# Conditioning columns in groups of four, parked FFN loads asked for earlier, and one operation for the FFN input's scale: a hybrid attention and SSD block on one core

## The chip, the cores and the metric

The kernel runs on one core of a Trainium2 chip. Five engines work side by side, each with its own queue: TensorE (PE, with its weight loads as PEld), VectorE (DVE), ScalarE (ACT), GpSimd (POOL) and SyncE (SP), whose queue here issues the DMAs. SBUF holds the tiles, PSUM the banks into which TensorE sums. The metric is the device time of one execution in microseconds; lower is better.

## The reference

One layer over x of 1024 rows and 1024 columns, all in float32. `mod` holds six vectors of 1024, made from a conditioning vector.

```python
mod = (jax.nn.silu(c) @ ada_w + ada_b)[:, None, :]
shift_m, scale_m, gate_m, shift_f, scale_f, gate_f = jnp.split(mod, 6, axis=-1)
h = rmsnorm(x, pre_norm_mix) * (1.0 + scale_m) + shift_m
proj = h @ w_in
...
y_a = sparse_mla_attention(q_lat, kv_lat, k_idx, w_idx, positions, ...) @ w_o_attn
y_b = ssd_mixer(z, xbc, dt_raw, ...) @ w_o_ssd
mix = (jax.nn.sigmoid(g_a) * y_a + jax.nn.sigmoid(g_b) * y_b) @ w_out
x = x + gate_m * rmsnorm(mix, post_norm_mix)
h2 = rmsnorm(x, pre_norm_ffn) * (1.0 + scale_f) + shift_f
u_gate, u_up = jnp.split(h2 @ w_ffn_in, 2, axis=-1)
f = (jax.nn.silu(u_gate) * u_up) @ w_ffn_out
x = x + gate_f * rmsnorm(f, post_norm_ffn)
```

The attention scores all keys with an indexer, keeps the best 256 per query and attends to these; the SSD mixer is a causal convolution of width 4 and a chunked scan.

## The kernel before

**Products.** Activations lie transposed: 128 channels in the partitions, rows in the free dimension, in two halves of 512 (`half(b)`, b = 0 and 1). A float32 product is made of split operands: hi is the rounded float32r copy (made by ACT), lo the rest (made by DVE or POOL), and three matmuls (hi with hi, lo with hi, hi with lo) add into one PSUM bank. Weights come through a stream of 128 x 4 x 128 pieces: SP loads wraw, ACT makes whi (L149), POOL makes wlo (L150), TensorE uses both.

**What sets the order.** The kernel is traced by Python, and a scheduler then orders each engine's queue by a simulated timetable. Under `in_order` a part keeps the written order on the named engines: TensorE through most of the attention, and again from the second half's output projection to the end of the early FFN tiles. Tiles lie in arenas of fixed slots (EV has 9 slots of 128 x 512, H 32, Q 26); a slot is given again when the last reader of its old tile is done. `bank_d` is a rotation of three PSUM banks, shared by the products pw, pos, pot, p2 and by adap.

**The conditioning columns.** `mod` has 48 columns of 128. Columns 16 to 47 are made beside the attention: `ada_slow` loads two adaw tiles of 256 KB, POOL multiplies both by the vector cs (L314) and adds them (L316), DVE reduces them to a tile adas of 128 x 128 (L318). `ada_next` keeps three columns waiting, and then `ada_col` multiplies one adas tile with a column of ones into a bank (L283), from which DVE adds the bias into `mod` (L284). Beside them stand `pw`, the products with w_in, whose convolution on DVE (cv, L892 to L894) reads two banks at a time.

**Merge and output projection.** `merge(b)` makes for each of eight blocks t a product pos with w_o_ssd; DVE multiplies it (mrg, L1138), POOL multiplies it by the gate (L1139), DVE adds the attention's part yal (L1142), and ACT and DVE split it into mg (L243, L244). `mixed(b)` multiplies the eight mg with w_out into pot. Then come the residual, the second normaliser and the FFN's input for this half.

**FFN input.** `residual_steps` ends with x1 times pr2, the normaliser spread over the partitions in PSUM (L1186). `ffn_input(b)` applies scale am2 and shift mod[24 + t]: for half 0 ACT makes h2h from x1 (L1195), DVE makes h2 in place (xr, L1196), and h2l is the difference (L1198, in turn on POOL and DVE). For half 1 only L1196 runs. Half 0's input is made during the last pos products of `merge(1)` and the first pot products.

**FFN tiles.** The FFN's first product uses Strassen's sums over four quarters. `early` makes the first products of 16 tiles (tile t's first half goes as p1, its gate part as g0, to a parking place d_p1 in DRAM) while the second half's residual is made; the list `fill` is this generator, `EARLY` is 16. `gate_up(t)` then does the rest of each tile: it loads four weight tiles a11, a12, a21, a22, loads the parked p1 and g0 (L1293, L1294), makes s1 and s2 (L1301, L1302), multiplies ("2", "1", "3", "22") and adds p1 into g1 (L1308). Weights become wr by ACT and POOL (L1251, L1252).

Of the kernel before, what the change touches and what calls it, by code (L numbers as in the profile page):

```python
# [10 lines left out]
F32 = mybir.dt.float32  # L11
F32R = mybir.dt.float32r
BF = mybir.dt.bfloat16
AF = mybir.ActivationFunctionType
OP = mybir.AluOpType
AX = mybir.AxisListType

P = 128
# [9 lines left out]
FT = D_FF // P  # L28
# [37 lines left out]
def build(tc, a, dbg=None, stop=99, slots=None):  # L66
    nc = tc.nc
    V, S, G, T, SP = nc.vector, nc.scalar, nc.gpsimd, nc.tensor, nc.sync
# [3 lines left out]
    con = ctx.enter_context(tc.tile_pool(name="con", bufs=1))  # L72
# [6 lines left out]
    EV = Arena(ctx, tc, "EV", n_slots["EV"], 512)  # L79
# [4 lines left out]
    def bank_d(name):  # L84
        return pd.tile([P, 512], F32, name=name, tag="d", bufs=3)

    def bank(name):
        return ps.tile([P, 512], F32, name=name, tag="s", bufs=5)

    def f(x):  # L90
        return x.bitcast(F32)
# [87 lines left out]
    def col(name, j=0, n=1):  # L179
        o, _ = COLS[name]  # L180
        return vec[:, o + j:o + j + n]
# [10 lines left out]
    onec = ones[:, 0:1]  # L192
# [15 lines left out]
    d_p1 = dr.tile([EARLY, 2, P, 512], F32, name="d_p1")  # L208
# [69 lines left out]
    mod = con.tile([P, 48], F32, name="mod")  # L278
    amul = con.tile([P, 8], F32, name="amul")

    def ada_col(j, acc):
        p = bank_d("adap")
        T.matmul(p[:, 0:1], acc, onec, start=True, stop=True)  # L283
        V.tensor_tensor(mod[:, j:j + 1], p[:, 0:1], col("ada_b", j), op=OP.add)  # L284

    cs32 = sm.tile([P, 8, 32], F32, name="cs32", tag="r2", bufs=1)
    V.memset(cs32, 0.0)
# [17 lines left out]
        V.tensor_tensor(mod[:, k:k + 9:8], p[:, 0:2], vec[:, k:k + 9:8], op=OP.add)  # L305
        V.scalar_tensor_tensor(amul[:, k:k + 1], mod[:, 8 + k:9 + k], 1.0, col("pre_mix", k), op0=OP.add, op1=OP.mult)

    def ada_slow(j):

        ts = []  # L310
        for h in range(2):
            t = wp.tile([P, 4, P], F32, name="adaw", tag="adaw", bufs=2)
            behind(SP.dma_start(t, a["ada_w"][j - 16][:, 4 * h:4 * h + 4]))
            behind(G.tensor_tensor(t, t, cs[:, 4 * h:4 * h + 4, None].to_broadcast([P, 4, P]), op=OP.mult))  # L314
            ts.append(t)
        G.tensor_tensor(ts[0], ts[0], ts[1], op=OP.add)  # L316
        acc = EV("adas", (P, P))
        V.tensor_reduce(acc, ts[0].rearrange("p k m -> p m k"), axis=AX.X, op=OP.add)  # L318
        return j, acc

    AHEAD = 4
    X0 = [[None, None] for _ in range(KT)]
    rx, Hs, first = [None, None], [([None, None], [None, None]) for _ in range(KT)], {}
# [62 lines left out]
    with in_order(*ORDERED, mybir.EngineType.SP):  # L386
        sums = [None, None], [None, None]
# [26 lines left out]
        for k in range(2, KT):  # L414
            k_h(k, 0)
            k_h(k, 1)
            if AHEAD <= k + 2 < KT:
                i = k_load(k + 2).ins
# [44 lines left out]
    for b in BS:  # L463
# [5 lines left out]
        hi, lo = Q("ksh", dt=F32R), Q("ksl", dt=F32R)  # L469
# [84 lines left out]
    acc = {i: (Q if i < 4 else R)(f"acc{i}") for i in range(QT0, NT)}  # L554
    for c in range(8):
# [5 lines left out]
        for hh in range(2):  # L561
            o, oo = 64 * hh, 64 - 64 * hh
            qs = []
            for b in BS:
                t = Q("qs", dt=F32R)
# [6 lines left out]
        for hh in range(2):  # L572
            qs = qss[hh]
            hd = 2 * c + hh
            for i in range(QT0, NT):
                n = (i + 1) * P
# [24 lines left out]
    for x in range(2):  # L601
# [3 lines left out]
        for j in range(NT):  # L605
# [3 lines left out]
            t = Q("v")  # L609
# [107 lines left out]
    if dbg is not None and "mk" in dbg:  # L717
        for i in MK:
            n = (i + 1) * P
            t = R("t")  # L720
# [175 lines left out]
            S.activation(ts[b], ts[b], AF.Silu)  # L896
            SP.dma_start(dst[:, half(b)], ts[b])

    slow, late = iter(range(16, 48)), []

    def ada_next():

        j = next(slow, None)
        if late and (j is None or len(late) > 2):
            ada_col(*late.pop(0))
        if j is not None:
            late.append(ada_slow(j))

    def group(g):
        return (16 + g, d_bc[g, 0]), (24 + g, d_bc[g, 1]), (2 * g, d_xs[2 * g]), (2 * g + 1, d_xs[2 * g + 1])  # L910
# [2 lines left out]
    for kind in FILL:  # L913
# [3 lines left out]
        elif kind == "z":  # L917
            t = next(n_z)
            gate(1 + t, d_z[t], AF.Silu)
        elif stop != 3:  # L920
            t = next(n_a)
# [177 lines left out]
    if stop <= 3:  # L1099
        for k in range(16):  # L1100
            for b in BS:
                t = EV("ydump")
# [9 lines left out]
    am2 = con.tile([P, 8], F32, name="am2")  # L1112
# [50 lines left out]
    def residual_steps(b, mix, sacc, x1):  # L1163

        r = rstd([sacc], D)
        yield
        prm = rspread(r)
        sacc = None
        for t in range(8):
            xr = Q("xr")  # L1170
            SP.dma_start(xr, a["xT"][t][:, half(b)])
            V.scalar_tensor_tensor(mix[t], mix[t], gm[:, t:t + 1], prm, op0=OP.mult, op1=OP.mult)
            (V if t % 2 else G).tensor_tensor(xr, mix[t], xr, op=OP.add)
            sq = mix[t]
            S.activation(sq, xr, AF.Square)
            if t:
                V.tensor_tensor(sq, sq, sacc, op=OP.add)
            sacc = sq
            x1.append(xr)
            SP.dma_start(d_x1[t][:, half(b)], xr)  # L1180
        yield
        r = rstd([sacc], D)
        yield
        pr2 = rspread(r)
        for t in range(8):
            V.tensor_tensor(x1[t], x1[t], pr2, op=OP.mult)  # L1186
        yield

    def ffn_input(b, x1):

        for t in range(8):
            h2 = x1[t]
            if b == 0:
                hi, lo = H_("h2h", dt=F32R), H_("h2l", dt=F32R)
                S.activation(hi, h2, AF.Identity, bias=mod[:, 24 + t:25 + t], scale=am2[:, t:t + 1])  # L1195
            V.tensor_scalar(h2, h2, am2[:, t:t + 1], mod[:, 24 + t:25 + t], op0=OP.mult, op1=OP.add)  # L1196
            if b == 0:
                (V if t % 2 else G).tensor_tensor(lo, h2, f(hi), op=OP.subtract)  # L1198
                X[("11", "21")[t // 4]][t % 4] = hi, lo
        return x1  # L1200


# [31 lines left out]
    x1 = []  # L1234
    for _ in residual_steps(0, *mixed(0, MG), x1):
        pass
    MG = merge(1, in_r)
    x1 = ffn_input(0, x1)


# [3 lines left out]
    def w_load(part, name, t, h):  # L1244
        r = w_tile(part, name)
        SP.dma_start(r, a["w_ffn_in"][t][:, 4 * h:4 * h + 4])
        return r
# [23 lines left out]
    def early(ts):  # L1271

        for t in ts:
# [10 lines left out]
            SP.dma_start(d_p1[t, 1], g)  # L1284
            yield

    def gate_up(t):

        a11, a12 = w_load(0, "a11", t, 0), w_load(0, "a12", t, 1)
        a21, a22 = w_load(1, "a21", FT + t, 0), w_load(1, "a22", FT + t, 1)  # L1290
        if t < EARLY:
            p, p1, g0 = bank("p0"), EV("p1"), EV("g0")
            SP.dma_start(p1, d_p1[t, 0])  # L1293
            SP.dma_start(g0, d_p1[t, 1])  # L1294
        else:
            p, g0, p2 = first_two(a11, a12)
            p1 = None
            V.tensor_tensor(g0, p2, g0, op=OP.add)
            S.activation(g0, g0, AF.Silu)
        s1, s2 = w_tile(2, "s1"), w_tile(2, "s2")  # L1300
        V.tensor_tensor(s1, a21, a22, op=OP.add)  # L1301
        V.tensor_tensor(s2, s1, a11, op=OP.subtract)  # L1302
        product(p, w_parts(s2), "2", p1 is not None)
        g1 = EV("g1")
        if p1 is None:
            S.activation(g1, p, AF.Copy)
        else:
            V.tensor_tensor(g1, p, p1, op=OP.add)  # L1308
        p5 = bank("p5")
        product(p5, w_parts(s1), "1", True)  # L1310
        u1 = EV("u1")
        if p1 is None:
            S.activation(u1, p5, AF.Copy)
        else:
            V.tensor_tensor(u1, p5, p1, op=OP.add)
        V.tensor_tensor(a21, a11, a21, op=OP.subtract)
        product(p, w_parts(a21), "3", False)
        V.tensor_tensor(u1, p, u1, op=OP.add)
        V.tensor_tensor(a12, a12, s2, op=OP.subtract)
        product(p5, w_parts(a12), "22", False)  # L1320
        V.tensor_tensor(g1, p5, g1, op=OP.add)
        S.activation(g1, g1, AF.Silu)
        top, j = t % 2 == 0, t // 2
        b12, t1 = kept[:, j % 2, 0], kept[:, j % 2, 1]
        last = b12 if top else g1
        V.tensor_tensor(last, g1, u1, op=OP.mult)
        if not top:
            SP.dma_start(d_a[PRODUCT["3"], j], g1)
            V.tensor_tensor(b12, g1, b12, op=OP.subtract)
            SP.dma_start(d_a[PRODUCT["7"], j], b12)  # L1330
            V.tensor_tensor(t1, g1, t1, op=OP.subtract)
            SP.dma_start(d_a[PRODUCT["6"], j], t1)
        product(p, w_parts(a22), "4", False)
        if p1 is None:
            V.tensor_tensor(g0, p, g0, op=OP.mult)
        else:
            V.tensor_tensor(p1, p, p1, op=OP.add)
            V.tensor_tensor(g0, g0, p1, op=OP.mult)
        if top:
            SP.dma_start(d_a[PRODUCT["1"], j], g0)  # L1340
            V.tensor_tensor(t1, b12, g0, op=OP.subtract)
            SP.dma_start(d_a[PRODUCT["5"], j], t1)
        else:
            SP.dma_start(d_a[PRODUCT["2"], j], g0)
            V.tensor_tensor(u1, g0, t1, op=OP.subtract)
            SP.dma_start(d_a[PRODUCT["4"], j], u1)

    kept = con.tile([P, 2, 2, 512], F32, name="kept", tag="mk")

    with in_order(mybir.EngineType.PE):  # L1350
        mix, sacc = mixed(1, MG)
        y1 = []
        fill, rest = early(range(EARLY)), residual_steps(1, mix, sacc, y1)
        for n in (2, 1, 7, 2):
            for _ in range(n):
                next(fill)
            next(rest)
        next(rest, None)
        ffn_sums(x1, ffn_input(1, y1))
        for _ in fill:  # L1360
            pass
    for t in range(FT):
        gate_up(t)

# [104 lines left out]
    with in_order(mybir.EngineType.PE, mybir.EngineType.Activation, mybir.EngineType.DVE,  # L1469
# [27 lines left out]
        for i, (name, j) in enumerate(steps):  # L1497
            n = ORDER.index(name)
# [14 lines left out]
            hi, lo = (alloc("a" + k, None, F32R) for k in "hl" for alloc in [(H_, Q)[PRODUCT[nxt] % 2]])  # L1513
# [23 lines left out]
        for c in BS:  # L1537
            cl, sacc = slice(256 * c, 256 * c + 256), None
            for m in range(4):
                p = bank("pfl")[:, 0:256]  # L1540
# [108 lines left out]
```

## Time and profile before

| what | value |
|---|---|
| time, median of 3 runs | 2430.15 us (2428.41 to 2433.94) |
| profiled execution | 2432.21 us |
| its span | 2430.3 us |
| mean granted TensorE clock | 0.991 |
| TensorE busy | 2352.2 us, 97% of the span |
| DVE, ACT, POOL busy | 65%, 50%, 44% |

The profiled execution takes 1.9 us more than its span, which is what lies around the recorded instructions. An engine's busy time is the sum of its instructions; what an engine waits for is told by the waits, which name the operation whose end released it. Times within the span are counted from its start.

### The profile page before, as it was taken

What the parts mean: (1) busy time and instruction counts of PE and PEld (TensorE: products, weight loads), DVE (VectorE), ACT (ScalarE), POOL (GpSimd) and SP (SyncE); (2) the same over time, 40 slices, a digit from 0 to 9 for tenths busy, and PEclk for the clock granted to TensorE, in tenths of its full rate; (3) what the DMA queues carried; (4) which work ended last, traced back from release to release, by engine and by line L of the source; (5) the groups of instructions that cost most, each with busy time, mean ns of one, the idle gap of its engine ahead of it and who ended that gap; (6) DMA issues with size and microseconds to landing.
All of it is one profiled execution on the core that took longest, in us unless ns stands there. A gap on an engine that the chain in (4) does not pass through costs nothing. (4 is left out here: it accounts for less than half of the span.)

```text
span 2430.3 us, 35062 instructions
## 1 busy us (share of the span) xinstructions
PE 2352.2 (97%) x11878; PEld 1909.0 (79%) x11878; DVE 1572.8 (65%) x3077; ACT 1226.1 (50%) x2336; POOL 1074.3 (44%) x854
## 2 busy tenths in 40 slices
PE   7999999999999999999999999999899999999997
PEld 5888888887888787777776777887777888887877
DVE  4466775598765566675557677354376877547776
ACT  4456665567455555455566565453444222335442
POOL 1422112222243446651345435666567555444465
PEclk9999999999999999999999999999999999999999
DMA  7123122522322223322668885554364555328664
GB/s 271 66 88 122 66 74 79 161 100 87 104 85 94 90 98 107 109 77 92 206 218 286 273 270 178 185 196 143 107 236 156 187 175 199 106 97 303 220 216 162
DMA packets 227651, 369.85 MB, mean 152 GB/s; under 512 B 22624, under 2 KB 84752, under 8 KB 227472
## 3 DMA queue, kind: packets, MB, share of 16 engines
q1 hardware_dynamic: 226752, 367.03, 45.1%
q8 instruction: 94, 1.54, 0.3%
q14 instruction: 85, 0.70, 0.1%
q10 hardware_dynamic: 720, 0.58, 0.1%
HBM read 275.74 MB, written 94.92 MB: 153 GB/s over the span
## 5 line engine op out<-in xcount | busy, mean ns | idle before, releaser
L150 POOL TENSOR_TENSOR wlo<-wraw,whi 128x512 fp32r<-128x512 f32 x242 | 331.4, 1371 | 612.6 <-ACT whi L149 558.2
L1258 PE MATMUL p<-xh,wr 128*128 128x512 f32 x880 | 276.6, 392 | 5.7 <-DVE g L1308 4.1
L149 ACT ACTIVATE whi<-wraw 128x512 fp32r<-128x512 f32 x242 | 151.1, 627 | 228.8 <-issue 58.0
L1252 POOL TENSOR_TENSOR wr<-a,wr 128x512 fp32r<-128x512 f32 x110 | 157.4, 1439 | 126.6 <-ACT wr L1251 94.0
L1258 PEld LDWEIGHTS p<-xh,wr 128*128 128x128 f32 x880 | 166.6, 189 | 41.7 <-DVE g L1308 4.6
L1258 PE MATMUL p<-xl,wr 128*128 128x512 f32 x440 | 172.2, 391 | 0.0
L778 ACT ACTIVATE lg<-lg,mx 128x256 f32<-128x256 f32 (+7 forms) x128 | 98.6, 772 | 93.8 <-DVE mx L775 91.5
L1251 ACT ACTIVATE wr<-a 128x512 fp32r<-128x512 f32 x110 | 68.4, 629 | 143.4 <-PE p L1258 120.8
L1258 PE MATMUL p<-h2h,wr 128*128 128x512 f32 x352 | 112.4, 395 | 0.0
L638 ACT ACTIVATE junk<-acc,cand__2182 128x1024 bf16<-128x1024 f32 (+2 forms) x96 | 86.2, 898 | 45.8 <-DVE cand__2182 L681 29.9
L314 POOL TENSOR_TENSOR adaw<-adaw,cs 128x512 f32<-128x512 f32 x64 | 66.3, 1041 | 90.5 <-DMA adaw<-ada_w 78.5
L1430 PE MATMUL pfo<-ah,wlo 128*128 128x512 f32 x264 | 103.4, 392 | 2.3 <-POOL wlo L244 2.3
L223 PE MATMUL pos<-yh,wlo 128*128 128x512 f32 x256 | 101.2, 396 | 2.8 <-POOL wlo L150 2.7
L1430 PE MATMUL pfo<-ah,whi 128*128 128x512 f32 x264 | 103.1, 390 | 0.7 <-ACT whi L243 0.7
L589 DVE SCALAR_TENSOR_TENSOR acc<-rel,widx,acc 128x384 f32<-128x384 f32 (+2 forms) x90 | 87.1, 988 | 24.9 <-ACT rel L584 24.7
L1430 PE MATMUL pfo<-al,whi 128*128 128x512 f32 x264 | 102.7, 389 | 0.0
L223 PE MATMUL pos<-yh,whi 128*128 128x512 f32 x256 | 101.1, 396 | 1.2 <-ACT yh L1124 1.2
L584 ACT ACTIVATE rel<-prel 128x512 f32<-128x512 f32 (+3 forms) x160 | 77.2, 523 | 48.5 <-PE prel L583 44.9
L223 PE MATMUL pos<-yw,whi 128*128 128x512 f32 x256 | 100.5, 393 | 0.0
L1258 PEld LDWEIGHTS p<-xl,wr 128*128 128x128 f32 x440 | 83.4, 189 | 17.3
L1519 DVE TENSOR_TENSOR al<-al,ah 128x512 fp32r<-128x512 f32 x66 | 73.1, 1110 | 36.1 <-ACT ah L1514 35.6
L799 PE MATMUL pt<-ident,lg 128*128 128x128 f32 x576 | 87.9, 277 | 4.0 <-ACT pc L804 2.1
(581 smaller groups left out, 7178.9 us busy)
## 6 DMA issues: line engine op xcount, KB each, us to landing
wraw<-w_in SPq DMA_DIRECT2D x130, 256.0 KB, 2.6
a<-w_ffn_in SPq DMA_DIRECT2D x120, 256.0 KB, 3.2
al<-d_a SPq DMA_DIRECT2D x77, 256.0 KB, 4.2
wraw<-w_ffn_out SPq DMA_DIRECT2D x66, 256.0 KB, 3.7
adaw<-ada_w SPq DMA_DIRECT2D x64, 256.0 KB, 2.7
al<-d_ac SPq DMA_DIRECT2D x32, 512.0 KB, 5.3
wraw<-w_o_ssd SPq DMA_DIRECT2D x64, 256.0 KB, 2.8
d_a<-kept SPq DMA_DIRECT2D x33, 256.0 KB, 3.0
```

The costliest lines, as they stand in the source:

```text
L149: behind(S.activation(hi[:, :kt], raw[:, :kt], AF.Copy))
L150: behind(G.tensor_tensor(lo[:, :kt], raw[:, :kt], f(hi[:, :kt]), op=OP.subtract))
L223: T.matmul(o, wt[:, k0 + i, :], xs[k][xi][b][:, sl], start=pi == 0 and i == 0 and wt is hi and xi == 0, stop=pi == len(pcs) - 1 and i == l ...
L584: S.activation(rel[:, 512 * b:512 * b + w_], pr[:, 0:w_], AF.Relu)
L589: V.scalar_tensor_tensor(acc[i][:, 0:n], rel[:, 0:n], ws, acc[i][:, 0:n], op0=OP.mult, op1=OP.add)
L638: S.activation(jk, y, AF.Sign, scale=-1.0, bias=a_, accum_out=o)
L778: S.activation(lg[:, 0:n], lg[:, 0:n], AF.Exp, scale=-1.0, bias=m, accum_out=mx[:, 3:4])
L799: T.transpose(ptv[:, hh, t, :], PR[hh, t][:, j * P:(j + 1) * P], ident)
L1252: G.tensor_tensor(w[:, 1], src, f(w[:, 0]), op=OP.subtract)
L1258: T.matmul(p, w[:, wi, i], X[x][i][xi], start=start and i == 0 and k == 0, stop=i == 3 and k == 2, skip_group_check=True)
L1430: T.matmul(o, w[wi][:, P * m:P * m + P], x[xi][:, cl], start=j == 0 and k == 0, stop=j == NP - 1 and k == 2)
L1519: V.tensor_tensor(lo, r, f(hi), op=OP.subtract)
```

## The change

Three edits.

1. Modulation columns end in fours. A tile of 128 x 4 x 128 in EV (first[j]) takes the reductions of four columns; `ada_cols` then makes four matmuls into one bank and one DVE add over four columns of `mod`. A group ends two columns after its last column is reduced.
2. `up_loads`, `parked` and `gate_loads` take the loads of `gate_up` out, and for tile 0 they are called behind steps 13, 15 and 17 of what is left of `fill`, beside the early tiles. `ahead` hands them on.
3. `residual_steps` multiplies by am2 and pr2 in one operation (a scalar_tensor_tensor, STT). `ffn_input` makes h2h with the shift alone on ACT, h2l on DVE alone (an STT that adds the shift and subtracts h2h), and h2 in place on ACT. The tensor_scalar of L1196 is gone.

```diff
-    def ada_col(j, acc):
+    def ada_cols(j, acc):
         p = bank_d("adap")
-        T.matmul(p[:, 0:1], acc, onec, start=True, stop=True)
-        V.tensor_tensor(mod[:, j:j + 1], p[:, 0:1], col("ada_b", j), op=OP.add)
+        for i in range(4):
+            T.matmul(p[:, i:i + 1], acc[:, i], onec, start=i == 0, stop=i == 3, skip_group_check=True)
+        V.tensor_tensor(mod[:, j:j + 4], p[:, 0:4], col("ada_b", j, 4), op=OP.add)
...
-    def ada_slow(j):
+    def ada_slow(j, acc):
...
-        acc = EV("adas", (P, P))
         V.tensor_reduce(acc, ts[0].rearrange("p k m -> p m k"), axis=AX.X, op=OP.add)
-        return j, acc
...
-    slow, late = iter(range(16, 48)), []
+    slow, sums = iter(range(16, 48)), {}
...
-        if late and (j is None or len(late) > 2):
-            ada_col(*late.pop(0))
+        if sums and (j is None or j % 4 == 2):
+            ada_cols(*sums.popitem())
         if j is not None:
-            late.append(ada_slow(j))
+            if j % 4 == 0:
+                first[j] = EV("adas", (P, 4, P))
+            acc = first[j - j % 4]
+            ada_slow(j, acc[:, j % 4])
+            if j % 4 == 3:
+                sums[j - 3] = acc
...
-            V.tensor_tensor(x1[t], x1[t], pr2, op=OP.mult)
+            V.scalar_tensor_tensor(x1[t], x1[t], am2[:, t:t + 1], pr2, op0=OP.mult, op1=OP.mult)
...
-                S.activation(hi, h2, AF.Identity, bias=mod[:, 24 + t:25 + t], scale=am2[:, t:t + 1])
-            V.tensor_scalar(h2, h2, am2[:, t:t + 1], mod[:, 24 + t:25 + t], op0=OP.mult, op1=OP.add)
-            if b == 0:
-                (V if t % 2 else G).tensor_tensor(lo, h2, f(hi), op=OP.subtract)
+                S.activation(hi, h2, AF.Identity, bias=mod[:, 24 + t:25 + t])
+                V.scalar_tensor_tensor(lo, h2, mod[:, 24 + t:25 + t], f(hi), op0=OP.add, op1=OP.subtract)
                 X[("11", "21")[t // 4]][t % 4] = hi, lo
+            S.activation(h2, h2, AF.Identity, bias=mod[:, 24 + t:25 + t])
...
+    def up_loads(t):
+        return w_load(1, "a21", FT + t, 0), w_load(1, "a22", FT + t, 1)
+
+    def gate_loads(t):
+        return w_load(0, "a11", t, 0), w_load(0, "a12", t, 1)
+
+    def parked(t):
+        p1, g0 = EV("p1"), EV("g0")
+        SP.dma_start(p1, d_p1[t, 0])
+        SP.dma_start(g0, d_p1[t, 1])
+        return p1, g0
...
-        a11, a12 = w_load(0, "a11", t, 0), w_load(0, "a12", t, 1)
-        a21, a22 = w_load(1, "a21", FT + t, 0), w_load(1, "a22", FT + t, 1)
+        a11, a12 = ahead.pop((gate_loads, t), None) or gate_loads(t)
+        a21, a22 = ahead.pop((up_loads, t), None) or up_loads(t)
...
-            p, p1, g0 = bank("p0"), EV("p1"), EV("g0")
-            SP.dma_start(p1, d_p1[t, 0])
-            SP.dma_start(g0, d_p1[t, 1])
+            p, (p1, g0) = bank("p0"), ahead.pop((parked, t), None) or parked(t)
...
-        for _ in fill:
-            pass
+        for i, _ in enumerate(fill):
+            for n, fn in ((13, up_loads), (15, parked), (17, gate_loads)):
+                if i == n:
+                    ahead[fn, 0] = fn(0)
```

What it moves in the queues, at the places that the prediction speaks of. First SP in the attention, beside the convolution (wraw are weight loads, adaw the column loads, d_att, d_bc stores of rb and cv). Before:

```order
L897 DMA d_bc_104<-cv_7008 128x512
L313 DMA adaw_7437<-ada_w 128x512
L148 DMA wraw_7678<-w_in 128x512
L820 DMA d_att_101<-rb_7177 128x256
L313 DMA adaw_7440<-ada_w 128x512
L148 DMA wraw_7898<-w_in 128x512
L313 DMA adaw_7663<-ada_w 128x512
L897 DMA d_bc_104<-cv_7205 128x512
```

After:

```order
L896 DMA d_bc_104<-cv_7002 128x512
L314 DMA adaw_7427<-ada_w 128x512
L314 DMA adaw_7430<-ada_w 128x512
L314 DMA adaw_7649<-ada_w 128x512
L314 DMA adaw_7652<-ada_w 128x512
L314 DMA adaw_7872<-ada_w 128x512
L314 DMA adaw_7875<-ada_w 128x512
L148 DMA wraw_7663<-w_in 128x512
L819 DMA d_att_101<-rb_7168 128x256
```

Six column loads now stand ahead of the weight load and the store of rb. This is so at two places of the attention; elsewhere four stand in a row at most.

Second DVE between the last two mrg of the second merge and the last mg. Before (xr is h2 of half 0):

```order
L1138 TENSOR_TENSOR mrg_16470<-pos_16397,rys_14669 128x512
L1196 TENSOR_SCALAR xr_15810<-xr_15810,am2_14553,mod_117 128x512
L1196 TENSOR_SCALAR xr_15816<-xr_15816,am2_14553,mod_117 128x512
L1142 TENSOR_TENSOR mrg_16470<-mrg_16470,yal_16476 128x512
L1198 TENSOR_TENSOR h2l_16573<-xr_15816,h2h_16572 128x512
L1196 TENSOR_SCALAR xr_15823<-xr_15823,am2_14553,mod_117 128x512
L244 TENSOR_TENSOR mg_16479<-mrg_16470,mg_16479 128x512
...
L1196 TENSOR_SCALAR xr_15844<-xr_15844,am2_14553,mod_117 128x512
L1198 TENSOR_TENSOR h2l_16593<-xr_15844,h2h_16592 128x512
L1138 TENSOR_TENSOR mrg_16555<-pos_16482,rys_14669 128x512
```

After:

```order
L1142 TENSOR_TENSOR mrg_16398<-pos_16325,rys_14597 128x512
L1200 SCALAR_TENSOR_TENSOR h2l_16496<-xr_15738,mod_117,h2h_16495 128x512
L1200 SCALAR_TENSOR_TENSOR h2l_16501<-xr_15744,mod_117,h2h_16500 128x512
L1200 SCALAR_TENSOR_TENSOR h2l_16506<-xr_15751,mod_117,h2h_16505 128x512
L1146 TENSOR_TENSOR mrg_16398<-mrg_16398,yal_16404 128x512
L1200 SCALAR_TENSOR_TENSOR h2l_16511<-xr_15758,mod_117,h2h_16510 128x512
L244 TENSOR_TENSOR mg_16407<-mrg_16398,mg_16407 128x512
L1200 SCALAR_TENSOR_TENSOR h2l_16516<-xr_15765,mod_117,h2h_16515 128x512
L1200 SCALAR_TENSOR_TENSOR h2l_16521<-xr_15772,mod_117,h2h_16520 128x512
L1142 TENSOR_TENSOR mrg_16483<-pos_16410,rys_14597 128x512
```

Six h2l stand between the two mrg where six L1196 and three L1198 stood; two more follow behind the second mrg, each ahead of a step of its mg. POOL has no h2l any more, and ACT has the eight in-place operations between its weight halves.

Third SP at the end of the early tiles. Before:

```order
L1246 DMA a22_17940<-w_ffn_in 128x512
L1284 DMA d_p1_109<-g0_17724 128x512
L1246 DMA a12_18049<-w_ffn_in 128x512
L1278 DMA d_p1_109<-p1_17751 128x512
L1246 DMA a11_18155<-w_ffn_in 128x512
L1246 DMA a21_18051<-w_ffn_in 128x512
L1284 DMA d_p1_109<-g0_17767 128x512
L1278 DMA d_p1_109<-p1_17794 128x512
L1293 DMA p1_17835<-d_p1_109 128x512
L1294 DMA g0_17836<-d_p1_109 128x512
```

After:

```order
L1249 DMA a22_17868<-w_ffn_in 128x512
L1298 DMA p1_17672<-d_p1_109 128x512
L1299 DMA g0_17673<-d_p1_109 128x512
L1287 DMA d_p1_109<-g0_17656 128x512
L1249 DMA a12_17977<-w_ffn_in 128x512
L1281 DMA d_p1_109<-p1_17687 128x512
```

The parked loads of tile 0 stand directly behind the a22 load of tile 1, seven places earlier. Tile 0's own a11, a12, a21 and a22 stood ahead of this place before, too.

More of the change, by code (lines that the diff above doesn't have):

```diff
@@ L1346, in gate_up @@
             SP.dma_start(d_a[PRODUCT["4"], j], u1)
-    kept = con.tile([P, 2, 2, 512], F32, name="kept", tag="mk")
+    kept, ahead = con.tile([P, 2, 2, 512], F32, name="kept", tag="mk"), {}
     with in_order(mybir.EngineType.PE):
```

## The prediction

> **What bounds the kernel now.** I read the page first, then the waits of TensorE, then the stretches around its long waits, then the rows of the engine that it waited for.
>
> ```profile
> span 2430.3 us, 35062 instructions
> PE 2352.2 (97%) x11878; PEld 1909.0 (79%) x11878; DVE 1572.8 (65%) x3077; ACT 1226.1 (50%) x2336; POOL 1074.3 (44%) x854
> ```
>
> TensorE (PE) is busy 97% of the span; 2430.3 - 2352.2 = 78.1 us are idle. The change removes no product, so it can win only these idle microseconds and the time that matmuls run slow behind them. The profiled execution took 2432.21 us (1.9 us around its span), 2.1 us more than the median 2430.15; I take the sum off the median.
>
> Who ends PE's waits, in the three stretches that the change touches (attention in written order, 650 to 900; attention left to the scheduler, 900 to 1146; from the end of the second merge into the FFN, 1690 to 1880):
>
> ```profile
> PE pw L233 <- DVE mod L284: 4.6, 4, 1.3
> PE pw L233 <- DVE cv L893: 0.4, 2, 0.2
> ...
> PE plg L766 <- DVE mx L775: 5.9, 5, 1.6
> ...
> PE p L1258 <- DVE g L1308: 4.1, 1, 4.1
> PE p L257 <- DVE mix L1177: 4.1, 1, 4.1
> PE pot L223 <- ACT mg L243: 3.8, 1, 3.8
> PE pot L223 <- DVE mg L244: 2.5, 1, 2.5
> PE p L1258 <- POOL wr L1252: 0.9, 1, 0.9
> PE p L1258 <- ACT wr L1251: 0.7, 1, 0.7
> ```
>
> (Total, times, longest.) A long wait costs more than itself, as the stretches of 5 us show; the number in brackets behind PE's busy time counts matmuls, and the third value from the end is the granted clock:
>
> ```profile
> 1715.00:1720.00 5.00, 2.78 (x7) 2.23 (x8) 2.16 (x2) 1.60 (x3) 2.21 (x2) 0.56 0.16 53
> 1720.00:1725.00 5.00, 5.00 (x18) 4.01 (x17) 0.00 (x0) 0.63 (x1) 1.37 (x2) 0.75 0.16 52
> 1725.00:1730.00 5.00, 5.00 (x24) 4.14 (x23) 0.92 (x1) 2.24 (x4) 2.16 (x2) 1.00 0.34 108
> ...
> 1870.00:1875.00 5.00, 5.00 (x12) 3.98 (x13) 3.19 (x5) 0.00 (x0) 0.00 (x0) 0.50 0.60 196
> 1875.00:1880.00 5.00, 5.00 (x21) 4.03 (x21) 1.84 (x3) 1.71 (x3) 2.54 (x2) 0.89 0.17 65
> ```
>
> At full clock 5 us hold 23 to 24 matmuls, about 0.215 us each. From 1720 to 1725 only 18 ran (1.2 us lost), and the 2.8 us busy before that held 7 instead of 13 (1.2): about 2.4 us behind the merge's waits. From 1870 to 1880 33 ran instead of 46 to 47, of which 13 x 0.215 = 2.8; say 2.5 belong to the 4.1 us wait.
>
> [...]
>
> **The change part by part.**
>
> *Ada columns by four.* Before, every column takes a bank of the rotation of three (bank_d) and gives it back by a mod add that stands in DVE's order behind the convolution. Afterwards two groups stand in the stretch 650 to 900, where the 4th and the 8th column stood. The four waits of 4.6 us fell at the 1st, 3rd, 5th and 7th column, where no group takes a bank any more; at the 4th and 8th PE waits 0.2 for cv, which stays. If the freed waits only move to the next product, half comes back; bounds 2.3 to 4.6. I take 4.2, since the next product's bank is then one turn older. The matmuls stay 64 records, the mod adds fall from 32 to 8 on a DVE that is 65% busy, nothing on the path. In 900 to 1146 the scheduler orders PE anew around the removed matmuls; the longest total there, 5.9 above, comes from the attention's own softmax, which stays. I take 0, with bounds of 4 us either way, two thirds of that wait.
>
> The loads move on SP: six adaw loads stand in a row where they stood singly between other transfers. I cost that at nothing; the cover is in these rows:
>
> ```profile
> SPq L148 <- POOL wlo L150: 135.8, 27, 12.4
> L316 POOL TENSOR_TENSOR adaw<-adaw 128x512 f32<-128x512 f32 x11 | 14.2, 1294 | 0.7
> L318 DVE TENSOR_REDUCE adas<-adaw x11: 1042/1068/1095, 688.5 to 892.6; 128x128 f32<-128x512 f32 x11
> L314 POOL TENSOR_TENSOR adaw<-adaw,cs 128x512 f32<-128x512 f32 x21 | 21.9, 1041 | 41.8 <-DMA adaw<-ada_w 35.4 <-DVE cv L894 4.8 <-DVE cv L892 1.7
> adaw<-ada_w SPq DMA_DIRECT2D x64, 256.0 KB, 2.7
> L819 DVE TENSOR_TENSOR rb<-po,rb x10: 413/417/425, 706.0 to 897.7; 128x256 f32<-128x256 f32 x10
> ```
>
> SP waits 135.8 of 245 us for weights to be consumed anyway, so weight loads stand far ahead. A column's round is 2.7 (landing) + 2 x 1.04 + 1.29 + 1.07 = 7.1 us, and six loads (two buffers) hold SP about two rounds, 14 us. What stands behind them is a d_att store of rb, whose single buffer is written again after (897.7 - 706.0) / 9 = 21.3 us. 7 us are left.
>
> *FFN input.* Rows of the end of the second merge: two of DVE, four of PE, then a stretch between the two mrg, and what the new forms cost elsewhere.
>
> ```profile
> 1694.81 0.69 DVE L1138 TENSOR_TENSOR mrg<-pos,rys 128x512 f32<-128x512 f32 x1 [5.38 <-PE pos L223]
> 1709.47 0.68 DVE L1138 TENSOR_TENSOR mrg<-pos,rys 128x512 f32<-128x512 f32 x1
> ...
> 1705.49 0.62 PE L223 MATMUL pot<-mg,whi 128*128 128x512 f32 x2
> 1710.02 0.39 PE L223 MATMUL pot<-mg,wlo 128*128 128x512 f32 x1
> 1714.20 0.50 PE L223 MATMUL pot<-mg,whi 128*128 128x512 f32 x1 [3.79 <-ACT mg L243]
> 1717.22 0.80 PE L223 MATMUL pot<-mg,whi 128*128 128x512 f32 x1 [2.52 <-DVE mg L244]
> ...
> 1695.45:1709.47 14.02, 14.02 (x63) 11.61 (x63) 13.20 (x13) 9.89 (x15) 12.10 (x8) 1.00 0.40 130
> ...
> L1196 DVE TENSOR_SCALAR xr<-xr,am,mod x16: 533/543/1519, 1696.1 to 1810.5; 128x512 f32<-128x512 f32 x16
> L1198 DVE TENSOR_TENSOR h2l<-xr,h2h 128x512 fp32r<-128x512 f32 x4 | 6.6, 1651 | 0.2
> L1125 DVE SCALAR_TENSOR_TENSOR yw<-yl,vec,yh x32: 734/751/1831, 1438.2 to 1591.6; 128x512 fp32r<-128x512 f32 x32
> L1172 DVE SCALAR_TENSOR_TENSOR mix<-mix,gm,prn x16: 740/742/748, 1624.5 to 1772.7; 128x512 f32<-128x512 f32 x16
> L1186 DVE TENSOR_TENSOR xr<-xr,prn x16: 678/680/689, 1659.0 to 1805.7; 128x512 f32<-128x512 f32 x16
> L1195 ACT ACTIVATE h2h<-xr,mod,am x8: 799/802/817, 1695.3 to 1706.0; 128x512 fp32r<-128x512 f32 x8
> L364 ACT ACTIVATE h2h<-x,mod x2: 722/724/725, 40.4 to 42.6; 128x512 fp32r<-128x512 f32 x2
> ```
>
> PE was through the last pos and began pot at 1705.5, but DVE came to the last mrg at 1709.47: nine operations of L1196 and L1198 stood ahead of it. POOL, DVE, ACT and DVE then made mg in turn, with two more of these operations before mg lo. Alone, DVE's work between the two mrg is 6 x 0.53 + 3 x 0.68 + yal and mg lo at 0.68 = 6.6 us (0.68 is the fastest two-operand row, L1186); it filled 13.2, beside eight POOL operations of about 1.3 (L316 above), 10.4: each us of POOL cost DVE 0.64. Afterwards six h2l STTs, yal and mg lo are 6 x 0.75 + 1.4 = 5.9, beside five POOL operations (three h2l are gone), 6.5: 5.9 + 0.64 x 6.5 = 10.1. So the mrg can start at 1695.5 + 10.1 = 1705.6, just as PE delivers; POOL takes 1.5, yal ends at 1709, ACT's mg at 1710, and mg lo, behind the last h2l, at 1711. PE wants it from 1710.4: a wait of 0.6 for 6.3, and no slow clock. Gain 5.7 + 2.4 = 8.1. Bounds: 8.7 with no wait; with every STT at L1125's slowest, 6 x 1.8 + 1.4 = 12.2, mrg is at 1707.7, the wait 2.2 and half the slow clock stays, 5.3.
>
> ACT loses 8 x 0.08 (0.80 to 0.72) and gains seven identities of 0.72, which follow each other every 0.65 or so, in these 14 us: 9.9 - 0.6 + 4.6 = 13.9. It is just full, so the weight halves come about 1 us later; PE holds more than one piece (2.7 us of matmuls) ahead, and I cost that at nothing. It is the thinnest cover of the sum.
>
> L1186 as STT costs 16 x 0.06 (0.742 against 0.680), in stretches where PE is fed by pot or early tiles. In the second half eight L1196 leave DVE just ahead of the FFN's sums, which start earlier; that counts only for the 1.6 us of the next part. The wait for L1177 stays.
>
> *Loads of main tile 0.*
>
> ```profile
> 1855.85 0.33 SPq L1246 DMA_DIRECT2D a<-w_ffn_in  x1
> 1864.39 0.43 SPq L1293 DMA_DIRECT2D p<-d_p  x1
> ...
> 1869.14 0.69 DVE L1308 TENSOR_TENSOR g<-p,p 128x512 f32<-128x512 f32 x1 [4.42 <-DMA p<-d_p]
> 1869.89 0.80 PE L1258 MATMUL p<-xh,wr 128*128 128x512 f32 x1 [4.13 <-DVE g L1308]
> ```
>
> The parked p1 is asked for at 1864.39 and used at 1869.14, 4.75 us later. Now its load stands directly behind the a22 load issued at 1855.85: used from 1861, g1 at 1861.7, before PE comes at 1869.89 - 4.13 = 1865.8, less what else was saved. The 4.1 and its 2.5 go. The 0.9 and 0.7 hang on s2 of tile 1, behind the FFN's sums; I take half, 0.8. The parked g0 behind p1 takes a slot that a DVE operation of an early tile gives back, done well before by the rotation; the two loads pass four stores and three weight loads, which come 0.4 us of issue later for each. Gain 7.4; bounds 8.2, and 4.1 if the next tile's load makes PE wait for half of it.
>
> Sum: 4.2 + 0 + 8.1 + 7.4 = 19.7; 2430.15 - 19.7 = 2410.5, said as 2411. All lower bounds together: 2.3 - 4 + 5.3 + 4.1 = 7.7 (2422); all upper: 4.6 + 4 + 8.7 + 8.2 = 25.5 (2405).
>
> **The rivals.**
>
> (A) *Slower: six adaw loads block SP.* If the columns keep the pace of before, 245 / 11 = 22.3 us, two rounds hold SP 44.6, and rb's next write waits 23.3 us on DVE, with the convolution and PE behind it; at two such places 46.6: 2411 + 46.6 = 2458. It outweighs the gain from rounds of (21.3 + 9.9) / 2 = 15.6 us. Against it: the operations themselves make 7.1.
>
> (B) *The merge stays bound by DVE or ACT.* If STT and POOL never overlap, 5.9 + 6.5 = 12.4 us and mrg is at 1707.9, mg lo at about 1713.2: a wait of 2.8 for 6.3, with half the slow clock, 3.4 us less gain, 2414; if ACT also falls 3 us behind, 2417. For it: L1198's mean of 1.65. [...] The stretch above goes against taking it in full: 13.2 busy us of DVE and 12.1 of POOL lay in 14.0, though the waits may be inside those busy times.
>
> (C) *Another wait takes the place of p1's*, for a22 or wr of tile 1 or for the next parked tile: the gain there is 3 for 7.4, 2415.
>
> (D) *The new order costs in 900 to 1146* and the columns win nothing: 19.7 - 4.2 - 4 = 11.5, 2419; with (C) 2423.
>
> **How the numbers follow.** Main case 0.55, 2411, its own range 2405 to 2417; B 0.12, C 0.10, D 0.13, A 0.10 (from a small block, 2425, to 2458). 0.2%, 4.9 us, is about what measurement tells from no change: faster is below 2425.3, slower above 2435. A gives half of itself to slower and half to the same, D with C a little to the same: faster 0.88, same 0.07, slower 0.05. From 2404 to 2425 lies about 0.85 of the chance; below 2404 more than all upper bounds would be needed.
>
> **What would show it.** Right: PE's waits for mod fall from 4.6 to about 0; mrg of the last pos starts within 1 us of PE's last pos, and no clock under 0.9 from 1700 to 1720; L1308's counterpart runs about 4 us before PE needs it, and 1860 to 1880 holds 0.9 or more. Wrong: a wait of PE for cv or rb of more than 3 us between 750 and 900 (A), mg still 2 us or more late (B), a wait for DMA p1 or a (C), or a sum of waits above 15 us in 900 to 1146 (D).

## The result, and the profile after

The changed kernel took 2417.56 us (median of 6 runs) against 2431.76 us for the kernel before beside it: a ratio of 0.9946, 95% interval 0.9931 to 0.9960, so 9.7 to 16.8 us faster. The prediction was 2411, 19.7 us faster, with a range of 2404 to 2425. The time fell by some two thirds of that.

The page after, its first rows:

```profile
span 2415.7 us, 35058 instructions
PE 2349.2 (97%) x11878; PEld 1907.3 (79%) x11878; DVE 1555.6 (64%) x3041; ACT 1234.1 (51%) x2352; POOL 1068.9 (44%) x850
```

TensorE is idle for 2415.7 - 2349.2 = 66.5 us, 11.6 less than before, and 3.0 us less busy with the same matmuls, which fits less slow clock behind long waits (mean granted clock 0.992 for 0.991). The waits of TensorE after, in the same three stretches (line numbers have moved by -1 in the attention, by 2 to 5 from the merge to the early tiles, by 13 in `gate_up`):

```profile
PE plg L765 <- DVE ql L737: 1.6, 3, 1.1
...
PE plg L765 <- DVE mx L774: 6.2, 6, 1.7
...
PE p L257 <- DVE mix L1181: 3.6, 1, 3.6
PE p L1261 <- DVE u L1328: 2.3, 1, 2.3
PE pot L223 <- DVE mg L244: 1.1, 1, 1.1
PE pot L223 <- ACT mg L243: 0.6, 1, 0.6
```

The waits for mod, for g and for wr are gone. Two have come: for ql in the attention, and for u at the FFN's begin.

Where the time went is read best from the start of each matmul in two traces. I matched the matmuls of both in order and took how much later or earlier the same one starts; the change of that shift over a stretch is what the stretch lost or won. The table has it for every kernel of this study against the profile of before, in us, with the stretches by the time of before. Each column is one profiled execution, and so is the profile of before: what that one lost or won by chance stands in every column. "ratio" is that of the timed runs.

| stretch | after | e1 | e2 | e3 | e4 | e7 | e8 | e10 | e11 | e12 |
|---|---|---|---|---|---|---|---|---|---|---|
| columns in | 4s | 4s | - | - | - | 4s | eight | eight | - | - |
| loads early | yes | - | yes | - | yes | yes | yes | yes | - | yes |
| FFN input new | yes | - | - | yes | yes | yes | yes | yes | yes | - |
| orders on DVE set | - | - | - | - | - | u1, mg | - | u1, mg | u1 | u1 |
| 0 to 660 | +1.3 | +0.9 | +0.1 | -1.6 | +0.8 | +0.6 | -1.3 | +3.0 | +0.7 | +0.9 |
| 660 to 900 | -3.1 | -3.3 | 0.0 | 0.0 | 0.0 | -3.7 | -4.1 | -4.1 | -0.1 | 0.0 |
| 900 to 1146 | +1.0 | +1.3 | -0.4 | -0.2 | -0.1 | +1.7 | +0.8 | +1.9 | +0.4 | -0.1 |
| 1146 to 1690 | -0.1 | -3.3 | -0.4 | -1.1 | +3.4 | -0.5 | +3.7 | +0.2 | -1.6 | +0.3 |
| 1690 to 1736 (merge) | -7.1 | -0.4 | -0.5 | -7.1 | -5.5 | -7.6 | -5.4 | -7.6 | -7.0 | +0.2 |
| 1736 to 1857 | -0.6 | -0.6 | -0.2 | -0.3 | -0.7 | +0.1 | -0.6 | -0.4 | -0.2 | +0.1 |
| 1857 to 2100 (FFN) | -6.8 | -1.8 | -2.5 | -5.3 | -6.6 | -9.5 | -7.1 | -9.5 | -5.4 | -7.5 |
| 2100 to the end | +0.8 | -0.4 | +2.0 | -1.0 | -0.1 | 0.0 | +0.1 | -0.8 | -0.2 | -1.1 |
| sum | -14.6 | -7.6 | -1.9 | -16.5 | -8.8 | -18.9 | -13.9 | -17.4 | -13.4 | -7.2 |
| ratio | 0.9946 | 0.9996 | 0.9993 | 0.9965 | 0.9950 | 0.9932 | 0.9939 | 0.9923 | 0.9953 | 0.9972 |

Rows 0 to 660, 1146 to 1690 and 2100 to the end hold nothing of the change but eight operations of the residual's new form from 1658 on, and they scatter by -3.3 to +3.7 us. So a column's sum says little (e1's is -7.6 where its timed runs show about none). The rows with the change repeat better between kernels that are alike there: -5.3 and -5.4, or -6.8, -6.6 and -7.1, or -9.5 and -9.5 at the FFN's begin. But they scatter too: the merge gives 7.1 and 5.4 with the same operations, and e1's FFN row shows -1.8 with none of the change in it. Both come mostly from the clock (1.6 of the 1.7 us between the two merges, 1.5 of e1's 1.8); the scatter has its own section at the end.

The rows that answer to the prediction's places. DVE and then PE at the end of the second merge:

```profile
1704.99 0.68 DVE L1142 TENSOR_TENSOR mrg<-pos,rys 128x512 f32<-128x512 f32 x1
1707.51 1.75 DVE L1146 TENSOR_TENSOR mrg<-mrg,yal 128x512 f32<-128x512 f32 x1 [1.19 <-POOL mrg L1143]
1709.19 1.75 DVE L1200 SCALAR_TENSOR_TENSOR h2l<-xr,mod,h2h 128x512 fp32r<-128x512 f32 x1
1710.87 0.68 DVE L244 TENSOR_TENSOR mg<-mrg,mg 128x512 fp32r<-128x512 f32 x1
...
1709.98 0.51 PE L223 MATMUL pot<-mg,whi 128*128 128x512 f32 x1 [0.56 <-ACT mg L243]
1711.61 0.50 PE L223 MATMUL pot<-mg,whi 128*128 128x512 f32 x1 [1.12 <-DVE mg L244]
```

The mrg starts at 1704.99; on the clock of before (this trace is 1.0 us ahead there) that is 1706.0, 3.5 us earlier than the 1709.47 of before. That is 0.7 us after the start of PE's last pos matmul (1704.28): the queue of FFN inputs hardly holds it any more. What is left is the way behind it: yal took 1.75 and the last h2l, which stands ahead of mg lo, another 1.75.

SP, DVE and PE at the FFN's begin:

```profile
1845.29 0.42 SPq L1298 DMA_DIRECT2D p<-d_p  x1
1855.47 1.59 SPq L1249 DMA_DIRECT2D a<-w_ffn_in  x2
...
1852.95 0.68 DVE L1321 TENSOR_TENSOR g<-p,p 128x512 f32<-128x512 f32 x1
1858.16 0.69 DVE L1314 TENSOR_TENSOR s<-a,a 128x512 f32<-128x512 f32 x1 [4.53 <-DMA a<-w_ffn_in]
1860.16 0.68 DVE L1328 TENSOR_TENSOR u<-p,p 128x512 f32<-128x512 f32 x1
...
1860.89 0.50 PE L1261 MATMUL p<-xh,wr 128*128 128x512 f32 x1 [2.29 <-DVE u L1328]
```

The parked p1 is asked for at 1845.29 and g1 is ready at 1853.6, with no wait. But DVE then stood 4.5 us at s1 of tile 2, whose a22 load was issued only at 1855.47, and u1 of tile 0 stood behind it in DVE's queue. That everything was there for u1 by then is shown by e7 below, where it ran right behind g1, at 1852.81. PE waited 2.3 us for u1.

### The profile page after: what moved, and what is told of

The parts are those of the page before. It is cut to its first block, busy times and chain, and to the rows that moved or that the text cites. A ratio compares the mean times of both kernels' runs of the same rounds, so it can differ in the third digit from the quotient of the medians.

```text
span 2415.7 us, 35058 instructions
## 1 busy us (share of the span) xinstructions
PE 2349.2 (97%) x11878; PEld 1907.3 (79%) x11878; DVE 1555.6 (64%) x3041; ACT 1234.1 (51%) x2352; POOL 1068.9 (44%) x850
## 5 line engine op out<-in xcount | busy, mean ns | idle before, releaser
L315 POOL TENSOR_TENSOR adaw<-adaw,cs 128x512 f32<-128x512 f32 x64 | 66.5, 1041 | 78.0 <-DMA adaw<-ada_w 65.8
```

## The experiments

**The parts alone.** e1_columns, e2_parked and e3_ffn_input are the kernel before with one of the three edits of the diff above, unchanged; e4_no_columns has the second and the third.

> Only the columns in fours; the FFN input and the parked loads are as before. Theory (the parts add up, each in its own stretch): the waits of pw for mod (4.6 us between 650 and 900) go, about 1.3 us come back as a wait for ql behind the convolution on DVE, and the stretch 900 to 1146 takes about 1.2 us longer by its new order; net 2 us faster than before, 2429.5 or so, hardly told from no change. Rival (the reordering costs as much as the waits gave): 0, with PE idle time in 900 to 1146 up by 3 us or more. Rival (six column loads in a row hold something up): slower, with a wait of PE for cv or rb over 3 us.

Measured: 0.9996 (0.9984 to 1.0008), 12 runs. That is between 3.9 us faster and 1.9 slower: it fits a gain of 2, or none, and not one of 4.2. By stretch: -3.3 between 660 and 900, +1.3 between 900 and 1146. The waits of PE between 655 and 900 were one row:

```profile
PE plg L765 <- DVE ql L737: 1.8, 3, 0.8
```

PE no longer waits for mod, 4.6 us, but meets DVE's convolution at the next product that needs DVE, 1.8 us. (The FFN's begin, -1.8 in e1's column, holds none of its edit and shows how far one profile can be off.) No wait for cv or rb is there, so the six column loads hold nothing up, though they hold SP for longer than estimated (SP in the changed kernel; 14.81 us at the second such place):

```profile
775.69 16.14 SPq L314 DMA_DIRECT2D adaw<-ada_w  x6
```

> Only the loads of the first main FFN tile asked for earlier. Theory: the wait of 4.1 us for g of L1308 and the slow clock of 2.5 us behind it go; a wait of about 2.3 us takes their place, for u1 of tile 0, which stands on DVE behind s1 of tile 1 and so behind that tile's a22 load: net 4 to 5 us faster, 2427. Rival (the early loads alone bring nothing without the FFN's sums being earlier): less than 2 us. Rival (the whole price, as predicted): 6.6 us, 2425.

Measured: 0.9993 (0.9984 to 1.0001), 11 runs, 1.7 us by the ratio, and -2.5 us in its stretch, little more than the -1.8 of e1, which has none of the edit. Less than the theory, and the first rival's size; that its reason is not the right one is shown by e12 below. (The wait that it names is there, but the expectation has the tile wrong: the order on DVE shows u1 of tile 0 behind s1 of tile 2, not of tile 1.) PE's waits and the slow clock at the FFN's begin:

```profile
PE p L1258 <- DVE u L1325: 3.2, 1, 3.2
PE p L1258 <- POOL wr L1252: 0.9, 1, 0.9
PE p L1258 <- ACT wr L1251: 0.5, 1, 0.5
...
1870.00:1875.00 5.00, 3.99 (x11) 3.19 (x12) 3.57 (x5) 1.00 (x2) 2.97 (x2) 0.66 0.40 143
```

The wait of 4.1 for g is gone, one of 3.2 for u1 has come, and the clock behind it is still slow: 11 matmuls in 4.0 us where 18 fit at 0.227 us each. PE's waits here are 4.6 us for 5.7 before, so 1.1 of the 2.5 is the edit's; the rest is nearly all a shorter slow clock (1.6 us for 3.1), as the next section shows.

> Only the FFN input's operations changed. Theory: the waits for mg at the end of the second merge fall from 6.3 to 1.7 us and the slow clock of 2.4 goes, 7.1 us; the 1.6 us of waits for wr of tile 1 go too, since the FFN's sums come earlier; the wait for g of L1308 (4.1 us) stays or grows by what was saved ahead of it: 7 to 9 us faster, 2424. Rival (the p1 load on SP stands behind stores that come no earlier, so PE waits there for what it saved before): 5.5 us or less.

Measured: 0.9965 (0.9952 to 0.9978), 5 runs, 8.5 us by the ratio (5.4 to 11.7); the merge gives 7.1 and the FFN's begin 5.3, though its loads are not moved in the code. The 12.4 of the two rows is above that interval: the profiled execution is the fastest of the five, 2415.72 for a median of 2424.61, with a mean granted clock of 0.994 where the others have 0.989 to 0.991. The rival's number, 5.5, is not clear of the interval, but what it says, that what is saved ahead is lost again at the p1 load, is out by the trace: the load is issued at 1851.55 for 1864.39 before, and PE's wait behind it is 3.6 us for 4.1. The one wait left at the FFN's begin, and the clock around it:

```profile
PE p L1257 <- DVE g L1307: 3.6, 1, 3.6
...
1855.00:1860.00 5.00, 3.04 (x13) 2.51 (x14) 2.42 (x4) 0.00 (x0) 1.71 (x2) 1.00 0.77 268
1860.00:1865.00 5.00, 5.00 (x23) 3.82 (x22) 3.35 (x6) 2.10 (x4) 3.42 (x3) 1.00 0.33 111
```

The waits for wr (1.6 us) are gone, since the FFN's sums came earlier (DVE ends the last of them at 1839.97 for 1856.37 before, 16.4 us earlier, where the matmuls come 10.3 earlier), and this wait of 3.6 us left the clock at 1.00.

> The FFN input and the parked loads as in the changed kernel, the columns one by one as before. Theory (parts add up): 14 - 2 = 12 us faster than before, 2419 to 2420. Rival (the columns bring their predicted 4.2 us): 10 us, 2422. Rival (the columns cost what they bring): as the changed kernel, 2417.

Measured: 0.9950 (0.9938 to 0.9962), 5 runs, 12.2 us by the ratio: the theory's 12. Beside the changed kernel's 13.1 it leaves the columns about 1 us, with intervals that overlap.

**What took the place of the p1 wait.** Two orders are set on DVE by a dependency that only orders, in the changed kernel (e7_both_first); with e8_eight_in_fours, and both in e10_all.

```diff
-        V.tensor_tensor(s1, a21, a22, op=OP.add)
+        s1i = V.tensor_tensor(s1, a21, a22, op=OP.add)
+        if t == 2:
+            after_(s1i, held["u1", 0])
...
-            V.tensor_tensor(u1, p5, p1, op=OP.add)
+            held["u1", t] = V.tensor_tensor(u1, p5, p1, op=OP.add)
...
+                if t == 7:
+                    after_(stt, held["lo"])
```

(held["lo"] is the last mg lo, stt the h2l operation; after_ adds the dependency.)

> The changed kernel with two orders fixed on DVE: s1 of the third main tile (tile 2) goes behind u1 of tile 0, and the last h2l of half 0 goes behind mg lo. Theory: the wait of PE for u1 (2.3 us, since s1 of tile 2 waits for its a22 load ahead of u1) goes, and the wait for mg lo (1.1 us) nearly goes: the stretch of the FFN's begin gives 2.3 us more, that of the merge's end 1.0 us more, 3 us faster than the changed kernel, 2414. Rival (a22 of tile 2 itself is what PE needs next): the 2.3 us come back as a wait for wr or s2 of tile 2 a product later; only 1 us faster. Rival (mg is held by ACT and POOL): the wait for mg stays at 1.5 us or more.

Measured: 0.9932 (0.9919 to 0.9944), median 2413.21, 3.4 us under the changed kernel's ratio, with intervals that overlap; the traces are clearer. The FFN's begin gives 9.5 where it gave 6.8, u1 starts at 1852.81 where it started at 1860.16, and no wait of PE is left between 1835 and 1890. The merge's waits:

```profile
PE pot L229 <- ACT mg L249: 0.6, 1, 0.6
PE pot L229 <- DVE mg L250: 0.5, 1, 0.5
```

1.1 us where 1.7 stood; the last h2l ahead of mg lo had cost 0.6, not 1.0. The rest hangs on yal and ACT.

> The kernel before with the loads of the first main FFN tile asked for earlier and s1 of tile 2 set behind u1 of tile 0 on DVE (as e2_parked with one order fixed). Theory (u1 behind s1 of tile 2, which waits for that tile's a22, is what took the place of the p1 wait): the wait of 3.2 us for u1 goes, the waits for wr (0.9 and 0.5) stay, no slow clock: the stretch gives 6 us instead of 2.5, 6 us faster than before, 2424 to 2425. Rival (a22 or wr of tile 2 takes the place at once): 2 to 3 us as e2_parked, with a new wait of about 3 us.

The second edit alone with u1's order set (e2_parked plus the first two pieces of the diff above). Measured: 0.9972 (0.9963 to 0.9982), 10 runs, 6.8 us by the ratio, and 7.5 in its stretch against e2's 2.5. PE's waits there:

```profile
PE p L1264 <- POOL wr L1258: 0.9, 1, 0.9
PE p L1264 <- ACT wr L1257: 0.5, 1, 0.5
```

So the p1 load has the predicted worth (4.1 and 2.5), without earlier sums, but only where u1 does not stand behind tile 2's load.

> The kernel before with the FFN input's operations changed and s1 of tile 2 set behind u1 of tile 0, the loads of the first main FFN tile and the columns as before. Theory (both are needed, p1's early load and u1's place): the wait for g (3.6 us, for p1) stays, and the time is that of e3_ffn_input, 0.35% under before, the stretch giving 5 us. Rival (the order alone does it and the early loads were not needed): the stretch gives 8 us or more and no wait over 1 us is left there.

The third edit alone with u1's order set. Measured: 0.9953 (0.9939 to 0.9966), 5 runs; by the ratio 11.4 us, more than e3's 8.5, with intervals that overlap, and 5.4 in the stretch, as e3's 5.3. The wait for g stays:

```profile
PE p L1263 <- DVE g L1315: 3.7, 1, 3.7
```

Both the early load and u1's place are needed for the 9.5; the order alone brings nothing in this stretch.

**The columns' loss between 900 and 1146.** In e8_eight_in_fours `ada_next` makes groups only of columns 16 to 23, and the other 24 go one by one:

```diff
+        if sums and (j is None or (j % 4 == 2 if sums[0][2] == 4 else len(sums) > 2)):
+            ada_cols(*sums.pop(0))
+        if j is not None and j < 24:
...
+        elif j is not None:
+            acc = EV("adas", (P, 1, P))
+            ada_slow(j, acc[:, 0])
+            sums.append((j, acc, 1))
```

> The changed kernel, but only the first eight columns in fours (the attention's part in written order); the other 24 end one by one as before. Theory: the stretch 650 to 900 keeps its gain of 3.1 us and the stretch 900 to 1146 loses its cost of 1.0 us, which comes from the scheduler's order around the missing single matmuls: 1 us faster than the changed kernel. Rival (the cost of 900 to 1146 comes with what the first stretch handed on, its earlier start against the same softmax chain): 900 to 1146 stays 1 us slower than before, as in the changed kernel.

Measured: 0.9939 (0.9927 to 0.9952), median 2415.38, not told from the changed kernel. 900 to 1146 still loses 0.8, and TensorE's order there is that of before, matmul for matmul, so this loss needs neither the missing single matmuls nor a new order; the rival stands so far. That what is won ahead is given back agrees with e7, whose order in this stretch is that of the changed kernel: it won 0.6 more ahead of 900 and lost 0.7 more behind it. It does not agree with e8 itself, which won 1.0 more than the changed kernel and lost 0.2 less. So the rival is not shown, and which step of the softmax chain sets the pace was not tried.

> Both orders fixed on DVE, and only the first eight columns in fours: the two kernels above in one. Theory: their stretches add up, 4 us faster than the changed kernel, 2413 to 2414, about 18 us under before. Rivals: as for the two, 1 to 2 us faster than the changed kernel.

Measured: 0.9923 (0.9910 to 0.9937), median 2412.24: 5.6 us under the changed kernel's ratio, the lowest of this study, 18.7 us under before; its interval overlaps e7's widely, so what the columns add here is not told. Its 1.9 between 900 and 1146 holds a slow clock behind a wait, 940.73 to 944.14, which e8, with the same matmuls there, did not have.

## Why the prediction was near, and where its steps failed

**The columns: 4.2 taken, 2.1 measured** (-3.1 and +1.0; e1 -2.0). Right that the waits for mod go altogether and that the six loads cost nothing: SP was held 16.1 and 14.8 us where 14 was estimated, still under the 21.3 of rb. The step that failed is "the next product's bank is then one turn older": the bank was free, but the next product that needs DVE's result, plg with ql, waited for the same convolution, 1.6 us. The prediction had named this ("the freed waits only move to the next product") and kept it for its lower bound. And 900 to 1146, taken as 0, gave back another 1.0; the bounds there, 4 either way, held it.

**The merge: 8.1 taken, 7.1 measured.** The mrg was forecast at 1705.6 and came at 1706.0 on that clock, but the step to it, "each us of POOL cost DVE 0.64", did not hold. DVE between the two mrg, and one of its three waits there:

```profile
1694.51:1704.99 10.48, 10.48 (x48) 8.67 (x47) 9.00 (x10) 10.20 (x18) 6.91 (x5) 1.00 0.45 143
...
1702.05 1.28 DVE L1200 SCALAR_TENSOR_TENSOR h2l<-xr,mod,h2h 128x512 fp32r<-128x512 f32 x1 [0.45 <-ACT h2h L1199]
```

By the forecast's own figures, 5.9 alone and POOL's 6.5, DVE's 9.0 busy us make (9.0 - 5.9) / 6.5 = 0.48. The 1.1 us by which DVE had less to do than the forecast's 10.1 were taken back by 1.4 us of waiting for ACT's h2h, which the forecast does not have: the two errors nearly cancel, which is luck. ACT was forecast just full and was, 10.20 busy of 10.48, and what that held up was DVE and not PE, which waited for no weight half. The wait left was 1.7 and not 0.6: yal and the last h2l, both beside POOL's weight halves, took 1.75 each where about 1.2 was put for yal. Rival B, with 2.8 left, was not the case. The new operations lie between the least and the most of L1125's row, but their median is 1.28 us where that row's is 0.75:

```profile
L1200 DVE SCALAR_TENSOR_TENSOR h2l<-xr,mod,h2h x8: 735/1276/1780, 1695.0 to 1709.2; 128x512 fp32r<-128x512 f32 x8
```

The sign "no clock under 0.9 from 1700 to 1720" held in the changed kernel, but not in e4 and e8, which have the same merge and clocks of 0.66 and 0.67 there; why is in the last section.

**The FFN's begin: 7.4 taken, 6.8 measured, and near by luck.** The step that failed is "The 4.1 and its 2.5 go": PE did come without waiting for g, but u1, one operation further, took its place, and 2.3 of the 4.1 came back. That is rival C, with a mechanism that it had not named: not a transfer that PE needed next, but an operation of DVE that was ready and stood behind one that was not. Two other terms made up for it. Of the waits for wr, where half of 1.6 was taken, all went. And the slow clock behind the waits of before, put at 2.5, was worth 3.1: PE ran 2.75 + 3.41 busy us at a clock of 0.50, of which half is taken as lost (its matmuls start 0.427 us apart there and 0.227 at 1.00). Before has the first two rows, e1 the third and e2 the fourth:

```profile
1869.23:1872.64 3.41, 2.75 (x7) 2.20 (x8) 2.07 (x4) 0.00 (x0) 0.31 (x1) 0.50 0.85 273
1872.64:1876.05 3.41, 3.41 (x10) 2.67 (x9) 2.35 (x5) 0.64 (x2) 0.00 (x0) 0.50 0.45 162
...
1863.89:1867.30 3.41, 3.19 (x8) 2.52 (x9) 2.02 (x4) 0.00 (x0) 0.30 (x1) 0.50 0.76 252
...
1870.77:1874.18 3.41, 3.17 (x8) 2.50 (x9) 2.80 (x4) 0.23 (x1) 2.75 (x2) 0.50 0.46 157
```

So 4.1 - 2.3 + 1.6 + 3.1 = 6.5 of the 6.8 us are placed. In e7, with the order set, the stretch gives 9.5, more than the 8.2 of the bound: 5.7 of waits, 3.1 of clock and 0.7 that is not placed. The clock also says why the parts do not add up. With u1's order set, the FFN input alone gives 5.4 (e11), the loads alone 7.5 (e12) and both 9.5: 3.4 less than the sum, since either alone ends the 3.1 of slow clock in its profile. And in e1 and e2 it cost 1.6 us where in before it cost 3.1; the difference is most of e1's 1.8, where nothing was changed, and more than half of e2's 2.5.

**Rivals A and D.** A is out: no wait for cv or rb. D, a loss of 4 between 900 and 1146, was a loss of 0.8 to 1.9 in the kernels with grouped columns, and 660 to 900 won 3.1 or more ahead of it.

The gap between 19.7 and the 14.6 of the two profiles is 5.1 us. The three parts make 2.1 + 1.0 + 0.6 of it; 2.1 more lie in the stretches ahead of 660 and behind 2100, which hold nothing of the change, and two other stretches give 0.7 back. By the ratio of the timed runs the gain is 13.1.

## What to carry to other kernels

When a wait is removed, ask which operation on the same engine comes next and what stands ahead of it in that queue: here an operation whose inputs were all there stood behind one that waited for a DMA, and setting that order took away the 2.3 us and gave the early load its worth. Gains of edits that end waits in one stretch need not add up: here 5.4 and 7.5 us alone made 9.5 together, because they shared one slow clock. Measure each alone and all together, and read them by the shift of the same matmul over a stretch, since the total of one profile scatters by as much as a part is worth (-3.3 to +3.7 us in stretches without the change). A bank freed earlier brought here only what the next result from DVE allowed, 2.1 us where 4.2 were taken.

## What the runs showed that was not expected

How much a wait costs beyond itself is not set by its length alone. The merge's end has the same two waits in the changed kernel and in e8 (0.6 and 1.1 us), with the same instructions behind them; the first row is the changed kernel's, the second e8's:

```profile
1710.00:1715.00 5.00, 3.88 (x16) 2.98 (x17) 1.55 (x2) 2.38 (x5) 1.69 (x2) 1.00 0.26 96
...
1710.00:1715.00 5.00, 3.84 (x9) 2.86 (x10) 1.60 (x2) 2.33 (x4) 1.73 (x2) 0.67 0.29 100
```

In 3.9 busy us 16 matmuls at clock 1.00 against 9 at 0.67: 7 matmuls of 0.23 us are 1.6 of the 1.7 us between the two merges in the table (-7.1 and -5.4; e4, at 0.66, has -5.5). And a wait of 3.6 us (e3) or 3.7 (e11) left the clock at 1.00, while one of 3.2 (e2) was followed by 0.66. Stretches that hold nothing of the change show it too. In both e1 and e8 PE waits 2.7 us for a weight half (wlo), up to 1640.13 in e1 and 1640.76 in e8; e1's row is the first, e8's the second:

```profile
1640.00:1645.00 5.00, 4.87 (x21) 4.05 (x22) 4.72 (x6) 1.87 (x4) 2.58 (x3) 1.00 0.31 105
...
1640.00:1645.00 5.00, 4.24 (x10) 3.41 (x11) 4.86 (x6) 1.78 (x3) 2.59 (x3) 0.50 0.31 108
```

What goes with a fall is in the traces. In each of them every fall of the clock lies on one grid of 3.41 us, to within 0.01, and the grid begins at another moment in each execution: from 80 to 2340 us, before has its falls at 1302.62, 1643.95, 1715.63, 1790.72 and 1869.23, and the changed kernel at 1300.69, 1642.03 and 1781.97. Cut on that grid, the merge's end in the changed kernel (first two rows) and in e8:

```profile
1706.88:1710.29 3.41, 2.85 (x13) 1.96 (x11) 2.78 (x2) 1.63 (x3) 3.41 (x3) 1.00 0.14 47
1710.29:1713.70 3.41, 2.29 (x10) 1.75 (x10) 1.26 (x2) 2.23 (x4) 0.91 (x2) 1.00 0.31 114
...
1708.28:1711.69 3.41, 1.71 (x8) 0.86 (x6) 3.32 (x3) 1.29 (x2) 2.17 (x2) 1.00 0.27 84
1711.69:1715.10 3.41, 3.41 (x8) 2.73 (x9) 0.00 (x0) 1.67 (x4) 1.28 (x1) 0.50 0.19 70
```

In e8 both waits fell into one piece of the grid, PE was busy for half of it, and the next piece ran at half the clock, 8 matmuls where a full one holds 16; in the changed kernel an edge of the grid lay between the two waits, and the clock stayed. So it is with the 3.6 us of e3, which the grid cuts into two pieces with 1.50 and 1.75 busy us. Over all eleven traces, from 80 to 2340 us and counting pieces at full clock, the clock halved right behind 35 of the 36 pieces in which PE was busy for less than 0.44 of the time, behind 7 of 25 from 0.44 to 0.52, and behind none of 7152 above; in before and the changed kernel alone it was 7 of 7, 1 of 6 and none of 1295. A forecast for this kernel can take the slow clock behind a wait as a chance, which I estimate from these counts to grow with the wait: where the grid will lie is not known ahead.
